# One decoder layer on one core: reordered ends of the sliding-window stage, block attention with one PSUM sum per tile, and a second place for one feed-forward factor

## The chip, the cores and the metric

The kernel is one program on one core of a Trainium2 chip. TensorE (PE) multiplies and transposes, VectorE (DVE), ScalarE (ACT) and GpSimd (POOL) work on tiles, SyncE (SP) and ACT issue the DMAs. The metric is the device time of one execution in microseconds (us). "Before" is the kernel without the change.

## The reference, cut to what matters

All data are float32, x is [1, 2048, 1024], one layer:

```
P = rms_norm(x) @ w_in                   # columns for the groups A (SWA), B (SSM), C (block attention)
A: 4 heads of 64, window 128, learned sinks, relative bias
B: S5 state-space model over 512 channels, then GELU and GLU
C: per query block of 128 (16 of them), 4 heads over one shared key/value head:
   o = g0 * softmax(q.k_cmp) v_cmp       # 127 compressed blocks; their probabilities pick the top 16 of 32 blocks
     + g1 * softmax(q.k_sel) v_sel       # keys of the selected blocks, others masked
     + g2 * softmax(q.k_win) v_win       # the last 512 keys
   k_cmp, v_cmp = gelu((blocks + pos) @ w1) @ w2
x = x + concat(rms_norm(o_A), rms_norm(o_B), rms_norm(o_C)) @ w_out
x = x + relu(rms_norm(x) @ w_up)^2 @ w_down      # w_up 1024 x 4096
```

## The kernel before, in words

A large product is made of three matmuls in fp32r (high x high, low x high, high x low; lines 76 to 78, and the same for the feed-forward at 1556 and 1738). Each operand is split in two: ACT writes the rounded high part, DVE the rest (`split`, lines 1414 and 1415).

*Front (0 to 418 us of the span).* x is normed and transposed, projected to the groups (`pm_a`, `pm_b`, `pm_c`, `pm_u`), and the state-space steps (`ssm_steps`) are merged between the last projection pieces; the last answer (`py`, lines 589 to 591) stands at the end.

*SWA, GLU, compress (418 to 611 us).* `merge` mixes three lists of steps in proportion: sliding-window attention, the GLU product of group B (`gpt` transposes, `gpm` products), and the preparation of group C with `compress_steps`. In the latter `cX` holds the tokens as two 512-column pieces, and `hidden` (line 765) reads it with a step of 8 elements: 16 fp32 matmuls `cph` of 129 columns per stream, two streams.

*Block attention and w_out (611 to 1304 us, `phase_mix`).* One tile is 128 queries. For each of three branches, `c` (compressed), `w` (window), `s` (selected): `logits` (line 875 on) makes q.k in PSUM (`pqc`, `pqw`, `pqs`; qA and qB are the two parts of the split query), DVE writes logits and their running maximum into a slab (`slc`, `slw`, `sls`, line 878; `nm..` is the last maximum), ACT takes the exponential of the whole slab and sums it (line 883, `den..`). `pv` transposes the slabs (`ppc`, `ppw`, `pps`, line 896), splits them (`th`, `tl`, lines 899 and 900), and multiplies by the values into a PSUM bank (`poc`, `pow`, `pos`, line 904). `combine` copies that bank to SBUF on ACT (`oT`, line 913), turns it back with four transposes (`pto.`, line 917), multiplies it by gate / denominator on DVE (`ot.`, line 919) and adds it to `oc` on POOL (lines 921 and 924). So each branch of each tile has its own bank, its own copy, four transposes, one DVE product and one to two POOL adds. A tile has four units: the heads 0 and 1, then 2 and 3, of `w`, then of `s`; the values of one unit are merged with the logits of the next unit. For tiles 8 to 15, `select` makes the mask of the top 16 blocks from the compressed probabilities; its transpose is `ptm` (line 1154), which goes into qB ahead of the selected logits. Between all this stand the products with w_out (`pw`, 48 matmuls per tile, placed with a priority offset), the norm of each finished tile (`xq`, `rr` on POOL), and the transposed rows for the feed-forward (`pth`).

*Feed-forward (1304 to 2572 us).* `phase_up` makes seven products per step in the manner of Strassen's method, in two halves of 16 steps f. The seven left factors ("1" to "7", order 1, 6, 7, 5, 2, 4, 3) are kept split in SBUF, one place for each. At the last step of half 0 each place is refilled for half 1 as soon as its product is done: "1" and "6" from fetched rows, the others landing by DMA in the place itself (`land`, then `split_landed`). `phase_down` follows.

The order on each engine comes from the order of these lists, from priority offsets (`late`), and from the pools, whose buffer counts decide what waits for a free place.

Of the kernel before, what the change touches and what calls it, by code (L numbers as in the profile page):

```python
# [80 lines left out]
def phase_front(tc, C, x, norm1_g, w_in, u_st, pd, rh_a, prm, dkp, dca, pre, extra, done):  # L81

    nc = tc.nc
    with ExitStack() as ctx:
# [165 lines left out]
        run(merge(rest, ssm_steps(tc, C, S, u_st, dkp, dca, tp, ps_g, ps_t)))  # L250
# [484 lines left out]
def compress_steps(tc, C, pool, tp, ps, pc, cmp_pos, cmp_w1, cmp_w2, gains):  # L735
# [7 lines left out]
    def start(st):  # L743
        X = box["X"] = tp.tile([P, 1040], F32, tag="X", name=f"cX{st}")
        nc.sync.dma_start(X[:, 1024:1040], cmp_pos[0, st].rearrange("(jj two) d -> (two d) jj", two=2))
        w1 = box["w1"] = tp.tile([P, 16, P], F32, tag="w1", name=f"cw1{st}")
        nc.sync.dma_start(w1, cmp_w1[0, st].rearrange("(jj p) f -> p jj f", p=P))
        w2 = box["w2"] = tp.tile([P, 64], F32, tag="w2", name=f"cw2{st}")
        nc.sync.dma_start(w2, cmp_w2[0, st])

    def turned(st, q):
# [6 lines left out]
        nc.scalar.copy(box["X"][:, 512 * q:512 * q + 512], pt.rearrange("p a b -> p (a b)"))  # L758

    def hidden(st):  # L760
# [3 lines left out]
        for jj in range(16):  # L764
            nc.tensor.matmul(ph, w1[:, jj], X[:, jj:jj + 8 * P + 1:8], start=jj == 0, stop=jj == 15)
# [80 lines left out]
class Attn:  # L846
# [12 lines left out]
    def logits(self, sl_of, h, qA, qB, chunks, m0, nm, den, name):  # L859
# [5 lines left out]
        def step(ci):  # L865
# [20 lines left out]
    def pv(self, po_of, sls_of, v_of, nblk, name):  # L886
# [3 lines left out]
        def step(b0):  # L890
            po, sls = po_of(), sls_of()
            nb = min(2, nblk - b0)
            pt = self.ps_p.tile([P, 2, 2, P], F32, tag="pp", name=f"pp{name}{b0}", bufs=2)
# [7 lines left out]
            for n, t in enumerate((th, tl)):  # L901
                with self.late(self.lag):
                    for j in range(nb):
                        nc.tensor.matmul(po, v_of(b0 + j), t[:, j].rearrange("p h q -> p (h q)"),  # L904
                                         start=b0 + j == 0 and n == 0, stop=b0 + j == nblk - 1 and n == 1)
        return [lambda b0=b0: step(b0) for b0 in range(0, nblk, 2)]

    def combine(self, po, w, acc, first, name, eng=None):
# [1033 lines left out]
```

## Time and profile before

| what | us |
|---|---|
| median of three runs | 2577.39 |
| lowest, highest run | 2571.80, 2578.93 |
| the profiled execution | 2574.28 |
| its span in the profile | 2572.5 |
| of which PE busy, DVE, ACT, POOL | 2475.1, 1769.6, 1324.9, 1119.3 |
| chain of waits: share spent on PE | 67% |

The profile is of one execution. Busy times of PE are sums over the stretches in which at least one matmul is in its pipeline, so short gaps between matmuls that depend on each other are partly counted as busy. A wait is put down to the semaphore that came last.

### The profile page before, as it was taken

What the parts mean: (1) busy time and instruction counts of PE and PEld (TensorE: products, weight loads), DVE (VectorE), ACT (ScalarE), POOL (GpSimd) and SP (SyncE); (2) the same over time, 40 slices, a digit from 0 to 9 for tenths busy, and PEclk for the clock granted to TensorE, in tenths of its full rate; (3) what the DMA queues carried; (4) which work ended last, traced back from release to release, by engine and by line L of the source; (5) the groups of instructions that cost most, each with busy time, mean ns of one, the idle gap of its engine ahead of it and who ended that gap; (6) DMA issues with size and microseconds to landing.
All of it is one profiled execution on the core that took longest, in us unless ns stands there. A gap on an engine that the chain in (4) does not pass through costs nothing.

```text
span 2572.5 us, 38493 instructions
## 1 busy us (share of the span) xinstructions
PE 2475.1 (96%) x12904; PEld 2080.1 (81%) x12904; DVE 1769.6 (69%) x3455; ACT 1324.9 (52%) x2767; POOL 1119.3 (44%) x1168
## 2 busy tenths in 40 slices
PE   8999998999999999999999999899999999999999
PEld 8989997777787777777777888688887888888887
DVE  4744876864787677777465565765557888888886
ACT  5334546765676565655465554544444444344442
POOL 3045222222223233332476767565545344454447
PEclk9999999999989999999999999999999999999999
DMA  6153426221212121221566667755547534444435
GB/s 199 61 126 102 116 89 172 86 60 50 65 64 71 36 67 48 87 66 56 177 204 187 187 185 207 233 163 144 153 130 251 167 93 136 132 132 130 123 98 197
DMA packets 397144, 324.66 MB, mean 126 GB/s; under 512 B 51943, under 2 KB 363885, under 8 KB 395121
## 3 DMA queue, kind: packets, MB, share of 16 engines
q1 hardware_dynamic: 360848, 297.03, 38.6%
q10 hardware_dynamic: 36096, 25.17, 3.1%
q8 instruction: 102, 1.67, 0.3%
q14 instruction: 98, 0.79, 0.1%
HBM read 209.66 MB, written 112.45 MB: 125 GB/s over the span
## 4 chain that ended last, share of the span: by engine, by line
PE 67%; DVE 5%; issue 2%; ACT 2%; DMA 2%; POOL 1%; SPq 0%; DVEq 0%; POOLq 0%; ACTq 0%
PE pdc L1738 7%; PE pdb L1738 7%; PE pda L1738 7%; PE pub L1556 6%; PE puc L1556 6%; PE pua L1556 6%; PE pdd L1738 3%; PE pud L1556 3%; PE pw L76 2%; PE pps L896 2%; PE pos L904 2%; PE pw L77 2%; PE pw L78 2%; DVE sls L878 1%; PE gpm L76 1%
## 5 line engine op out<-in xcount | busy, mean ns | idle before, releaser
L1414 ACT CAST v<-vr 128x512 fp32r<-128x512 f32 x224 | 139.4, 624 | 304.2 <-DMA vr<-vd 148.4
L1415 DVE TENSOR_TENSOR v<-vr,v 128x512 fp32r<-128x512 f32 x224 | 233.1, 1048 | 81.2 <-ACT v L1414 79.2
L1738 PE MATMUL pdc<-dw,v 128*128 128x512 f32 x768 | 187.0, 392 | 4.3 <-ACT dw L1414 3.2
L1738 PE MATMUL pdb<-dw,v 128*128 128x512 f32 x768 | 185.2, 390 | 0.0
L1738 PE MATMUL pda<-dw,v 128*128 128x512 f32 x768 | 184.5, 389 | 0.0
L1527 POOL TENSOR_TENSOR fs<-ur,ur 128x512 f32<-128x512 f32 x64 | 94.8, 1481 | 189.2 <-DMA ur<-in_w_up 152.0
L1738 PEld LDWEIGHTS pdc<-dw,v 128*128 128x128 f32 x768 | 145.3, 189 | 35.4 <-ACT dw L1414 3.7
L1738 PEld LDWEIGHTS pdb<-dw,v 128*128 128x128 f32 x768 | 144.8, 189 | 30.3
L1738 PEld LDWEIGHTS pda<-dw,v 128*128 128x128 f32 x768 | 144.1, 188 | 30.0
L1414 ACT CAST uh<-fs 128x512 fp32r<-128x512 f32 x128 | 78.5, 621 | 152.0 <-PE pub L1556 62.7
L1415 DVE TENSOR_TENSOR ul<-fs,uh 128x512 fp32r<-128x512 f32 x128 | 134.3, 1051 | 22.6 <-ACT uh L1414 22.3
L1415 DVE TENSOR_TENSOR ul<-ur,uh 128x512 fp32r<-128x512 f32 x96 | 101.0, 1053 | 52.3 <-ACT uh L1414 48.5
L900 DVE TENSOR_TENSOR tls<-pps,ths 128x512 fp32r<-128x512 f32 (+1 forms) x144 | 93.2, 658 | 46.0 <-ACT ths L899 37.7
L899 ACT CAST ths<-pps 128x512 fp32r<-128x512 f32 (+1 forms) x144 | 79.5, 565 | 83.4 <-PE pos L904 40.3
L76 PE MATMUL pw<-wo_h,mh 128*128 128x512 f32 x256 | 109.2, 427 | 6.2 <-ACT mh L1251 4.2
L1572 POOL TENSOR_TENSOR ev<-e,e 128x512 f32<-128x512 f32 x64 | 95.9, 1498 | 31.9 <-ACT e L1569 21.9
L1556 PE MATMUL pua<-fh,ul 128*128 128x512 f32 x256 | 100.9, 394 | 5.7 <-DVE ul L1415 5.7
L78 PE MATMUL pw<-wo_h,ml 128*128 128x512 f32 x256 | 105.4, 412 | 0.0
L77 PE MATMUL pw<-wo_l,mh 128*128 128x512 f32 x256 | 105.1, 410 | 0.0
L1556 PE MATMUL puc<-fh,uh 128*128 128x512 f32 x256 | 102.1, 399 | 1.9 <-DVE eu L1565 1.9
L1556 PE MATMUL pub<-fh,uh 128*128 128x512 f32 x256 | 102.1, 399 | 1.6 <-ACT fh L1414 1.6
L1556 PE MATMUL pua<-fh,uh 128*128 128x512 f32 x256 | 101.0, 395 | 2.5 <-ACT e L1576 2.5
(573 smaller groups left out, 7875.3 us busy)
## 6 DMA issues: line engine op xcount, KB each, us to landing
vr<-vd SPq DMA_DIRECT2D x224, 256.0 KB
ur<-in_w_up SPq DMA_DIRECT2D x128, 256.0 KB
vd<-ev SPq DMA_DIRECT2D x128, 256.0 KB
vd<-e ACTq DMA_DIRECT2D x64, 256.0 KB
dr<-in_w_down SPq DMA_DIRECT2D x32, 512.0 KB
x<-in_x SPq DMA_DIRECT2D x16, 512.0 KB
mx<-in_x SPq DMA_DIRECT2D x16, 512.0 KB
x<-mx ACTq DMA_DIRECT2D x16, 512.0 KB
```

Source lines behind the costliest of these rows:

```text
L76: nc.tensor.matmul(out, sh, mh, start=first, stop=False)
L77: nc.tensor.matmul(out, sh, ml, start=False, stop=False)
L78: nc.tensor.matmul(out, sl, mh, start=False, stop=last)
L896: nc.tensor.transpose(pt[:, j, hh], sls[hh][:, (b0 + j) * P:(b0 + j + 1) * P], C["ident"])
L899: nc.scalar.copy(th[:, 0:nb], pt[:, 0:nb])
L900: nc.vector.tensor_tensor(tl[:, 0:nb], pt[:, 0:nb], th[:, 0:nb], op=ALU.subtract)
L1414: nc.scalar.copy(dh, src)
L1415: nc.vector.tensor_tensor(dl, src, dh, op=ALU.subtract)
L1527: nc.gpsimd.tensor_tensor(t, x, y, op=op)
L1556: nc.tensor.matmul(bank[b], w[:, k], h[o][:, k], start=first and k == 0 and n == 0, stop=k == HALF - 1 and n == 2, skip_group_check=True)
L1572: nc.gpsimd.tensor_tensor(tile_("v" + o), x, y, op=op)
L1738: nc.tensor.matmul(bank[b, q], x[:, q, j], y[:, j], start=first and j == 0 and n == 0, stop=j == 1 and n == 2, skip_group_check=True)
```

## The change

1. Front: the last four projection pieces (48 matmuls `pm_c`) come after the last state-space step. The lists at the end of the SWA stage are merged in another proportion: six empty steps follow compress.
2. Compress: `cX` is laid out so that `cph` reads 129 neighbouring columns; ACT writes it in that layout, and the position row comes in two DMAs per stream.
3. Block attention: right after each exponential, DVE takes the reciprocal of that head's sum and POOL multiplies the whole slab by reciprocal x gate (line 887 of the changed kernel). All three branches then sum in one bank `poc` per tile, which a tile opens with its compressed values; one copy, four transposes and one DVE `tensor_reduce` give `oc`. The window slabs get a tag of their own. The values are merged with the logits of the unit after next. PSUM: three `pp` banks and one `po` bank instead of two and two.
4. Small edits in the same stage: two reciprocal square roots go from DVE to POOL, a square is written to SBUF instead of PSUM, `next_turned` stands later in the list of a tile.
5. Feed-forward: half 1's factor "1" has a place of its own (16 KB per partition), fetched and split at step 14; "6" and "7" are both refilled from fetched rows at step 15. One square per step goes from DVE to ACT.

```diff
-        run(merge(rest, ssm_steps(tc, C, S, u_st, dkp, dca, tp, ps_g, ps_t)))
+        run(merge(rest[:-4], ssm_steps(tc, C, S, u_st, dkp, dca, tp, ps_g, ps_t)) + rest[-4:])
...
-        nc.scalar.copy(box["X"][:, 512 * q:512 * q + 512], pt.rearrange("p a b -> p (a b)"))
+        nc.scalar.copy(box["X"][:, :, 64 * q:64 * q + 64], pt.rearrange("p a (m j) -> p j (a m)", j=8))
...
-            nc.tensor.matmul(ph, w1[:, jj], X[:, jj:jj + 8 * P + 1:8], start=jj == 0, stop=jj == 15)
+            nc.tensor.matmul(ph, w1[:, jj], X[:, jj % 8, jj // 8:jj // 8 + P + 1], start=jj == 0, stop=jj == 15)
...
                 nc.scalar.activation(x, x, AF.Exp, bias=nm[:, h:h + 1], scale=-1.0, accum_out=den[:, h:h + 1])
+                if gate is not None:
+                    nc.vector.reciprocal(den[:, h:h + 1], den[:, h:h + 1])
+                    nc.gpsimd.tensor_scalar(x, x, den[:, h:h + 1], gate, op0=ALU.mult, op1=ALU.mult)
...
+                        opening = b0 + j == 0 and n == 0 and first is not None
+                        begun = first.get("mm") if opening else None
+                        with self.tc.issue_after(begun) if begun is not None else nullcontext():
+                            mm = nc.tensor.matmul(po, v_of(b0 + j), t[:, j].rearrange("p h q -> p (h q)"), start=opening and begun is None,
+                                                  stop=last and b0 + j == nblk - 1 and n == 1, skip_group_check=True)
...
+        if w is None:
+            nc.vector.tensor_reduce(acc, pt.rearrange("p h a d -> p h d a"), axis=AX.X, op=ALU.add)
+            return
...
-        ps_p = pool("m_psp", 2, space=PSUM)
-        ps_o = pool("m_pso", 2, space=PSUM)
+        ps_p = pool("m_psp", 3, space=PSUM)
...
+        ps_o = pool("m_pso", 1, space=PSUM)
...
+                if i >= 8:
+                    pn = box["pn"] = lp.tile([P, 4, P], F32, tag="qd", name=f"pn{i}", bufs=1)
+                    nc.gpsimd.tensor_tensor(pn[:, :, 0:n], slc[:, :, 0:n], den.unsqueeze(2).broadcast_to([P, 4, n]), op=ALU.mult)
+                nc.gpsimd.tensor_tensor(slc[:, :, 0:n], slc[:, :, 0:n], w.unsqueeze(2).broadcast_to([P, 4, n]), op=ALU.mult)
...
-                def close(box=box, nm_=nm_, b=b, den=den, w=w):
-                    nc.vector.reciprocal(den, den)
-                    nc.vector.tensor_tensor(w, den, gt[:, :, b], op=ALU.mult)
-                    A.combine(box["po"], w, oc, False, f"{nm_}{i}", nc.vector if (nm_, i) == ("w", NT - 1) else None)
...
+                    if end and pair == 1:
+                        ps.append(lambda: A.combine(po(), None, oc, f"c{i}"))
...
+            for u in range(4):
+                if u == 2 and i + 1 < NT:
+                    ocs[i + 1] = box["oc"]
+                    nxt = units_of(i + 1, box)
...
+                new = cur[u + 2][0] if u < 2 else nxt[u - 2][0] if nxt else []
+                run(merge(cur[u][1], new, ahead[done_a:na], tail[done_t:nt]))
...
+        factors(ORDER[:1], "t")
+        second, hp["1"] = hp["1"], first
...
-                nc.vector.tensor_tensor(r, r, r, op=ALU.mult)
+                nc.scalar.activation(r, r, AF.Square)
...
+            if (p, f) == (0, NF - 2):
+                hp["1"] = second
+                fetch_factor(1, "1")
             if last:
-                for o in ORDER[:2]:
+                for o in ORDER[1:3]:
                     fetch_factor(1, o)
...
+                if (p, f) == (0, NF - 2) and k == 4:
+                    again = refill(1, "1")
```

What stands on PE between the front and the SWA stage, in the kernel before (`py15` is the last answer of the state-space steps, `pm15_c` the last projection piece, `ptqa` a transpose of SWA queries that POOL makes as `qda`, `bpfs` the bias of SWA, `gpt` transposes for the GLU; the last digits are running numbers of the program):

```order
L78 MATMUL pm15_c0_4856<-wh_c0_7_4323,hl15_2484 128x396
L589 MATMUL py15_4895<-Wc15_4787,U15_4802 128x256
L590 MATMUL py15_4895<-Wc15_4787,U15_4802 128x128
L591 MATMUL py15_4895<-CA15_4786,St1_3076 128x256
L589 MATMUL py15_4895<-Wc15_4787,U15_4802 128x256
L590 MATMUL py15_4895<-Wc15_4787,U15_4802 128x128
L591 MATMUL py15_4895<-CA15_4786,St1_3076 128x256
L712 MATMUL bpfs0_4983<-Ts_4981,c_anti_4936 128x512
L647 MATMUL gpt0_5084<-c_ident_60,z0_5082 128x128 x3
L825 MATMUL ptqa0_4994<-c_ident_60,qda0_4992 128x128 x3
```

And in the changed kernel, from the last projection piece on:

```order
L78 MATMUL pm15_c0_4872<-wh_c0_7_4383,hl15_2484 128x396
L647 MATMUL gpt0_5084<-c_ident_60,z0_5082 128x128 x4
L712 MATMUL bpfs0_4983<-Ts_4981,c_anti_4936 128x512
L647 MATMUL gpt1_5472<-c_ident_60,z1_5470 128x128 x2
L712 MATMUL bpfs2_4986<-Ts_4981,c_anti_4936 128x512
L647 MATMUL gpt1_5472<-c_ident_60,z1_5470 128x128 x2
L712 MATMUL bpf00_5058<-T0_5056,c_anti_4936 128x512
L76 MATMUL gpm01_5509<-glu_h_4974,zh0_5089 128x512
L77 MATMUL gpm01_5509<-glu_l_4975,zh0_5089 128x512
L78 MATMUL gpm01_5509<-glu_h_4974,zl0_5090 128x512
L76 MATMUL gpm01_5509<-glu_h_4974,zh0_5089 128x512
L826 MATMUL ptqa0_4994<-c_ident_60,qda0_4992 128x128 x4
```

The answer has moved ahead of the last projection pieces, and products of the GLU stand between them and the first SWA transpose.

On DVE, in block attention at tile 12 of the changed kernel, after the logits of head 0 of the selected branch (`nms12` its maximum, written by the rows of line 879; `qB1` is the low part of tile 13's query, `kAs` the keys):

```order
L879 ISA sls120_13200,nms_12852<-pqs1203_13269,b_sel_4941,mx_13199 128x512
L879 ISA nms_12852 128x1
L904 TENSOR_TENSOR tlw1200_13286<-ppw1200_13280,thw1200_13285 128x512
L833 SCALAR_TENSOR_TENSOR qB1_7405<-ptqc13_13299,gains_62,qA13_13304 64x512
L879 ISA sls121_13329,mx_13328<-pqs1210_13330,b_far_4945 128x512
L879 ISA mx_13328 128x1
L886 RECIPROCAL dens_12853<-dens_12853 128x1
L839 SCALAR_TENSOR_TENSOR kAs_7400<-ptkc13_13307,gains_62,kAs_7400 64x128
```

In the kernel before one reciprocal of all four heads stood at the end of the branch; here each head has its own, three operations behind its maximum.

On DVE at the change of halves in the feed-forward (`fl16` is the low part of factor "6" of half 1, `ul105` the low part of weights of half 1 for product "5", `e` and `eu` results of products), in the kernel before:

```order
L1415 TENSOR_TENSOR fl11_19047<-fx11_19027,fh11_19046 128x2048
L1565 TENSOR_TENSOR eu2015_19063<-pud015_19050,e1015_19031 128x512
L1415 TENSOR_TENSOR fl16_19066<-fx16_19029,fh16_19065 128x2048
L1565 TENSOR_TENSOR eu3015_19082<-puc015_19069,eu2015_19063 128x512
L1415 TENSOR_TENSOR ul106_19203<-fs102_19200,uh106_19202 128x512
L1565 TENSOR_TENSOR e22015_19100<-pub015_19087,eu3015_19082 128x512
L1415 TENSOR_TENSOR ul107_19209<-fs103_19206,uh107_19208 128x512
L1415 TENSOR_TENSOR ul105_19213<-fs101_19198,uh105_19212 128x512
L1415 TENSOR_TENSOR fl17_19085<-fl17_19085,fh17_19084 128x2048
L1592 TENSOR_TENSOR e11015_19110<-e11015_19110 128x512
L1565 TENSOR_TENSOR e21015_19143<-puc015_19069,eu2015_19063 128x512
L1415 TENSOR_TENSOR fl15_19106<-fl15_19106,fh15_19105 128x2048
```

And in the changed kernel:

```order
L1575 TENSOR_TENSOR eu2015_18864<-pud015_18851,e1015_18836 128x512
L1421 TENSOR_TENSOR ul106_19003<-fs102_19000,uh106_19002 128x512
L1421 TENSOR_TENSOR fl16_18867<-fx16_18832,fh16_18866 128x2048
L1575 TENSOR_TENSOR eu3015_18883<-puc015_18870,eu2015_18864 128x512
L1421 TENSOR_TENSOR fl17_18886<-fx17_18834,fh17_18885 128x2048
L1575 TENSOR_TENSOR e22015_18902<-pub015_18889,eu3015_18883 128x512
L1421 TENSOR_TENSOR ul107_19009<-fs103_19006,uh107_19008 128x512
L1421 TENSOR_TENSOR ul105_19013<-fs101_18998,uh105_19012 128x512
L1421 TENSOR_TENSOR ul102_19017<-ur1012_18992,uh102_19016 128x512
L1575 TENSOR_TENSOR e21015_18943<-puc015_18870,eu2015_18864 128x512
L1421 TENSOR_TENSOR fl15_18908<-fl15_18908,fh15_18907 128x2048
```

The split of "1" is gone from here (it stands some thirty rows earlier), that of "7" reads fetched rows (`fx17`) and stands ahead of the weight splits, and the square of line 1592 is on ACT.

## Rows read from the trace of the kernel before

**Rows 1.** The page: span, and (columns: engine, busy us, share, instructions) the busy line.

```profile
span 2572.5 us, 38493 instructions
...
PE 2475.1 (96%) x12904; PEld 2080.1 (81%) x12904; DVE 1769.6 (69%) x3455; ACT 1324.9 (52%) x2767; POOL 1119.3 (44%) x1168
```

**Rows 2.** Stages of the program as windows (columns: window, its length, then busy us of PE, PEld, DVE, ACT, POOL with the count of instructions, granted clock of PE as a share of full speed, DMA share, GB/s). In order: front; SWA, GLU and compress; block attention and w_out; up; down.

```profile
0.00:418.00 418.00, 402.37 (x2584) 385.14 (x2584) 247.12 (x608) 194.90 (x403) 120.07 (x200) 1.00 0.40 116
418.00:611.00 193.00, 175.88 (x985) 140.35 (x985) 125.88 (x377) 123.36 (x376) 49.42 (x54) 0.98 0.32 93
611.00:1304.00 693.00, 651.51 (x3898) 536.26 (x3899) 497.77 (x1449) 420.90 (x1023) 235.31 (x467) 0.97 0.24 75
1304.00:1951.00 647.00, 632.90 (x2753) 512.42 (x2752) 387.42 (x425) 330.54 (x560) 403.42 (x274) 0.99 0.61 178
1951.00:2572.50 621.50, 612.47 (x2688) 505.87 (x2686) 511.37 (x600) 255.24 (x407) 311.07 (x175) 0.99 0.47 146
```

**Rows 3.** PE in block attention, 611 to 1304 us, by groups (columns: line, engine, operation, out<-in, shapes, count; busy us and mean ns of one; idle us just before them and what ended it).

```profile
L76 PE MATMUL pw<-wo_h,mh 128*128 128x512 f32 x256 | 109.2, 427 | 6.2 <-ACT mh L1251 4.2 <-DVE ml L1252 1.4 <-ACT pw L1267 0.3
...
L896 PE MATMUL pps<-c_ident,sls 128*128 128x128 f32 x544 | 93.1, 278 | 4.5 <-DVE tls L900 2.0 <-ACT sls L883 1.4 <-DVE rat L52 0.3
...
L875 PE MATMUL pqs<-kAs,qA 128*128 128x512 f32 (+3 forms) x160 | 66.1, 413 | 7.2 <-DVE mx L878 5.6 <-DVE nms L878 1.0 <-DVE nmc L878 0.3
...
L896 PE MATMUL ppw<-c_ident,slw 128*128 128x128 f32 x280 | 57.0, 292 | 1.7 <-DVE nmc L878 0.7 <-ACT slw L883 0.5 <-DVE tls L900 0.2
...
L1249 PE MATMUL ptx<-c_ident,mix 128*128 128x128 f32 x128 | 20.8, 286 | 3.3 <-ACT pw L1267 1.7 <-DVE ml L1252 1.3 <-ACT mx L1287 0.2
...
L1284 PE MATMUL pth<-c_ident,mx 128*128 128x128 f32 x64 | 12.4, 287 | 2.9 <-POOL mx L1276 2.9
L917 PE MATMUL ptos<-c_ident,oTs 128*128 128x128 f32 x64 | 11.2, 291 | 2.0 <-ACT oTs L913 1.9
L917 PE MATMUL ptow<-c_ident,oTw 128*128 128x128 f32 x64 | 10.8, 279 | 0.2
```

**Rows 4.** The chain of waits, 505 to 625 us (columns: start us, us, engine, tile, line, count).

```profile
507.77 0.44 PE ptoa L917 x4
...
521.35 7.64 PE cph L765 x32
...
584.01 3.37 issue
...
588.12 7.74 PE cph L765 x32
```

**Rows 5.** Two fp32 products, all their matmuls (columns: line, engine, operation, out<-in, count; shortest/median/longest ns; first and last start; form). The first has neighbouring columns, the second a step of 8.

```profile
L590 PE MATMUL py<-Wc,U x64: 272/274/275, 266.9 to 416.3; 128*128 128x128 f32 x64
...
L765 PE MATMUL cph<-cX,cw x64: 412/413/478, 521.3 to 595.4; 128*128 128x129 f32 x64
```

**Rows 6.** ACT, then DVE in block attention, by groups (columns as in Rows 3).

```profile
L883 ACT ACTIVATE sls<-sls,nms 128x128 f32<-128x128 f32 (+15 forms) x64 | 77.5, 1211 | 23.6 <-DVE nms L878 21.9 <-DVE im L1146 1.6
L883 ACT ACTIVATE slw<-slw,nmw 128x640 f32<-128x640 f32 (+4 forms) x64 | 49.0, 766 | 19.5 <-DVE nmw L878 19.3
...
L883 ACT ACTIVATION_READ_ACCUMULATOR sls<-sls,nms 128x1 f32 x64 | 12.5, 195 | 0.0
...
L913 ACT COPY oTs<-pos 128x512 f32<-128x512 f32 x16 | 9.4, 585 | 3.7 <-PE pos L904 3.6
...
L919 DVE TENSOR_TENSOR ots<-ptos,ws 128x512 f32<-128x512 f32 x16 | 11.0, 687 | 6.1 <-PE ptos L917 6.1
...
L1141 DVE TENSOR_REDUCE pm<-pn 128x72 f32<-128x288 f32 (+7 forms) x8 | 7.0, 871 | 1.5 <-POOL pn L1140 1.3
...
L1129 DVE RECIPROCAL denc<-denc 128x4 f32<-128x4 f32 x16 | 2.8, 173 | 1.3 <-ACT slc L883 1.1
```

**Rows 7.** POOL in block attention, by groups (columns as in Rows 3).

```profile
L924 POOL TENSOR_TENSOR oc<-oc,ots 128x256 f32<-128x256 f32 x32 | 23.5, 735 | 79.9 <-DVE ots L919 77.0 <-DVE denw L1182 1.7
L924 POOL TENSOR_TENSOR oc<-oc,otw 128x256 f32<-128x256 f32 x30 | 22.6, 754 | 41.9 <-DVE otw L919 25.7 <-DVE wc L1132 9.3 <-DVE im L1145 3.8
...
L921 POOL TENSOR_TENSOR oc<-otc 128x256 f32<-128x256 f32 x16 | 11.8, 735 | 82.2 <-DVE otc L919 82.2
...
L1276 POOL TENSOR_SCALAR mx<-mx,rr 128x1024 f32<-128x1024 f32 x8 | 8.9, 1118 | 0.8
...
L1239 POOL TENSOR_SCALAR mix<-mix,r_a 128x256 f32<-128x256 f32 x16 | 7.6, 477 | 2.6 <-DVE r_c L54 2.6
```

**Rows 8.** Four windows of 20 us: the start of the SWA stage, and the change of halves (columns as in Rows 2).

```profile
420.00:440.00 20.00, 14.49 (x72) 10.17 (x73) 15.33 (x45) 16.40 (x45) 6.21 (x5) 0.91 0.80 214
1600.00:1620.00 20.00, 20.00 (x89) 16.25 (x88) 12.91 (x12) 12.93 (x18) 15.02 (x10) 1.00 0.55 152
1620.00:1640.00 20.00, 18.51 (x79) 14.47 (x78) 13.22 (x12) 9.94 (x12) 8.43 (x5) 1.00 0.85 311
1640.00:1660.00 20.00, 11.81 (x43) 8.86 (x42) 20.00 (x17) 10.62 (x15) 12.83 (x7) 0.83 0.73 225
```

**Rows 9.** The change of halves: a row of the chain of waits, then rows of the order of events on DVE (columns: start us, us, engine, line, operation, out<-in, count, and in brackets the idle time before it).

```profile
1624.77 6.03 DMA fl<-sums
...
1632.77 2.29 DVE L1415 TENSOR_TENSOR fl<-fl,fh 128x2048 fp32r<-128x2048 f32 x1 [6.78 <-ACT fh L1414]
...
1642.86 3.35 DVE L1415 TENSOR_TENSOR fl<-fl,fh 128x2048 fp32r<-128x2048 f32 x1
```

More of the change, by code (lines that the diff above doesn't have):

```diff
@@ L743, in start @@
     def start(st):
-        X = box["X"] = tp.tile([P, 1040], F32, tag="X", name=f"cX{st}")
-        nc.sync.dma_start(X[:, 1024:1040], cmp_pos[0, st].rearrange("(jj two) d -> (two d) jj", two=2))
+        X = box["X"] = tp.tile([P, 8, 130], F32, tag="X", name=f"cX{st}")
+        for b in range(2):
+            nc.sync.dma_start(X[:, :, 128 + b], cmp_pos[0, st, 16 * b:16 * b + 16].rearrange("(jj two) d -> (two d) jj", two=2))
         w1 = box["w1"] = tp.tile([P, 16, P], F32, tag="w1", name=f"cw1{st}")
@@ L857, in late, with logits @@
         return self.tc.high_priority(offset=-n) if n else nullcontext()
-    def logits(self, sl_of, h, qA, qB, chunks, m0, nm, den, name):
+    def logits(self, sl_of, h, qA, qB, chunks, m0, nm, den, name, gate=None):
         nc = self.nc
@@ L1118, in slab @@
                 return slc
-            def po():
-                if "po" not in box:
-                    box["po"] = ps_o.tile([P, 512], F32, tag="po", name=f"poc{i}")
-                return box["po"]
             res = []
@@ L1266, in out @@
                     box["ss"] = small(2, "xs")
-                nc.scalar.activation(pw, xt, AF.Square, accum_out=box["ss"][:, n:n + 1])
+                nc.scalar.activation(late["fp"].tile([P, 512], F32, tag="sq", name=f"xsq{i}{n}"), xt, AF.Square, accum_out=box["ss"][:, n:n + 1])
                 if n == 1:
@@ L1315, in finish_steps @@
             res = [load, lambda: turned(0, 4), lambda: turned(4, 8)] + [lambda n=n, k=k: filler(n, k) for n, k in order]
+            before = late.pop("turn", [])
+            res[8:8] = before
             if i >= NT // 2:
-                res.insert(8, blocks)
-                res.insert(13, block_sums)
-            res[1:1] = late.pop("turn", [])
+                res.insert(8 + len(before) * 3, blocks)
+                res.insert(13 + len(before) * 3, block_sums)
             if i < NT // 2:
@@ L1329, in front, with po @@
             box = {}
+            def po():
+                if "po" not in box:
+                    box["po"] = ps_o.tile([P, 512], F32, tag="po", name=f"poc{i}")
+                return box["po"]
+            box["po_of"] = po
             def start():
@@ L1446, in phase_up @@
         factors(ORDER[3:])
+        first = hp["1"]
+        factors(ORDER[:1], "t")
+        second, hp["1"] = hp["1"], first
         ps_u = pool("f_psu", 2, space=PSUM)
@@ L1504, in refill @@
         def refill(p, o):
-            hh[o], hl[o] = (hp[o].tile([P, HALF, 4, P], F32R, tag=n + o, name=f"f{n}{p}{o}") for n in "hl")
-            split(nc, hh[o], hl[o], rows.pop(o))
+            t = [hp[o].tile([P, HALF, 4, P], F32R, tag=n + o, name=f"f{n}{p}{o}") for n in "hl"]
+            split(nc, *t, rows.pop(o))
+            return t
         def weights(p, f):
@@ L1616, in phase_up @@
             if k < 2:
-                refill(0, o)
+                hh[o], hl[o] = refill(0, o)
             else:
```

108 lines of the change are left out of this document (47 added, 61 removed).

## The prediction

> **What bounds the kernel.** I read the stages first [rows 2]. PE is busy in 402 of 418 us, 176 of 193, 652 of 693, 633 of 647 and 612 of 622; no other engine comes near, the closest being DVE in block attention with 498 of 693. PE's order is the bound everywhere, and a change pays in two ways: work that PE no longer does, and gaps on PE that close. The visible gaps are 16, 17, 41, 14 and 9 us. Two stages have most of them, so I looked at those two group by group [rows 3] and at the chain through the stage before them [rows 4]. In the feed-forward one place stands out: of the windows of 20 us [rows 8] a full one holds 89 matmuls, and the two at the change of halves hold 79 and 43. That is 56 missing, and at 20/89 = 0.225 us each 12.6 us, nearly the whole gap of that stage.
>
> The sum is made against the profiled execution, 2574.28 us, of which the span is 2572.5 [rows 1]; the median of the three runs is 3 us higher, their lowest 2.5 us lower.
>
> **Block attention, removed work on PE.** Two of three turns per tile go: 2 x 16 x 4 = 128 transposes (`ptos`, `ptow`, 64 each [rows 3]). Four of them in a row take 0.44 us when nothing holds them, the first of [rows 4], so 32 x 0.44 = 14.1 us of PE's order. They also waited 2.0 and 0.2 us for the copies. This is -16 and nearly sure, because it stands on the engine that bounds.
>
> **Block attention, waits that may close.** The values now come two units behind the logits. Waiting for the slab or its split parts cost the transposes `pps` 4.5 and `ppw` 1.7 us [rows 3]; the part of these that hangs on the exponential should go, the part that hangs on `tls` (2.0) not. PE's wait of 7.2 us before `pqs` is for DVE to free the logits' bank, and DVE is hardly lighter: it loses 48 products of 0.687 us (33 us) and small products and reciprocals of 14 us at most (64 at about 0.2), and gains 128 reciprocals of at most 0.173 (22 us) and 16 reduces of about 0.87 (14 us) [rows 6]. That is 498 - 33 - 14 + 22 + 14 = 487 us. ACT loses 32 copies of 0.585, 19 of 421 us [rows 2, 6], which frees the casts a little. For these waits I take -4, with bounds of -25 (all of the 41 us of gaps but the 16 that I ascribe to other causes, the logits and w_out) and +20 (below).
>
> **Block attention, the new work on POOL.** The gates multiply all slabs. Window slabs have min(i+1, 5) blocks of 128, selected ones i+1, times four heads: 35,840 and 69,632 elements per partition over 16 tiles. POOL's products with a scalar took 477 ns at 256 elements and 1118 at 1024 [rows 7]: 0.835 ns per element over about 0.263 us fixed. So 128 x 0.263 + 105,472 x 0.000835 = 34 + 88 = 122 us. The 16 products of the compressed slabs add about 10 (from the adds of 0.735 for 256 elements). Gone are 11.8 + 23.5 + 22.6 = 58 us of adds. POOL goes from 235 to about 309 of 693 us, 45%. It is hidden by the distance of two units, except where a gate queues behind POOL's chain for a finished tile (eight small operations and a product of 1.118) or where three gates of late tiles of 1.5 to 2 us follow one another. A missed one costs PE one or two us unless w_out products fill in. I take +2, bounds 0 and +15.
>
> **Block attention, single bank and selection.** With one `po` bank, the first compressed value of a tile must wait for the copy of the tile before (0.585 us [rows 6] plus the drain of the last product). That happens 15 times, with w_out products to fill: +3, bounds 0 and +12. In the order of the changed kernel the mask of tiles 8 to 15 stands close in front of its logits; eight times a part of a chain of small DVE operations: +2, bounds 0 and +8. The edits of group 4 take the square away from the bank that w_out waits for (`ptx` 1.7 us, `pw` 0.3, both on ACT `pw`) and let `mx` be ready before `pth` (2.9) [rows 3]: -3 of 4.9, bounds -5 and +2. The moved square roots are small and early; POOL's queue hides them, and uncovered they would cost a few us once.
>
> Block attention sums to -16 - 4 + 2 + 3 + 2 - 3 = -16. Since the waits that the profile names hide drains which it counts as busy (four transposes that wait for a copy take the bank, the copy and the turn in sequence), I put it at -22, with -50 and +8 as ends. The addition of 6 is judgement: every dependent step that is taken off PE's order lets its neighbours pipeline.
>
> **Compress.** The 64 `cph` take 413 ns, a contiguous fp32 product of nearly the same size 274 [rows 5]; their two runs on the chain took 7.64 + 7.74 = 15.4 us [rows 4]. If the step of 8 elements is what makes the difference, 64 x 0.139 = 8.9 us go; the odd 129th column keeps a little, so -8. If it is the odd column itself, nothing goes: bounds -9 and 0. The writes of ACT now scatter, eight of them, off the chain.
>
> What decides between the two is a rule: the Trainium skill, "SBUF — State Buffer", section "Door 1: The DMA port swizzle", states that SBUF is read in lines of 16 bytes and that each access to a new line pays. The step of 8 fp32 values is 32 bytes, a new line each time. By that rule the sum has -8, without it 0. The longer `cph` rows agree with it but don't exclude the odd column.
>
> **Front and SWA.** PE is busy for 14.49 of the first 20 us at a granted clock of 0.91 [rows 8], waiting for queries that POOL and DVE prepare. In the new order GLU products stand there, work that came later anyway; the last answer is made earlier, so its `z` is there. I take -3 of the 5.5 us. The 3.37 us of issue ahead of the second `cph` [rows 4] is a wait for loads that the earlier placing may hide: -2. Bounds for both together -9 and +3 (the projection pieces now end later, and the stores and loads of SWA's tiles stand behind them on SP's queue).
>
> **Change of halves.** PE waits there for DVE, which is busy for all 20 us from 1640 [rows 8]. It stood idle for 6.78 us before 1632.77, because the split of "7" waited for a DMA of 6.03 us [rows 9], and then did splits of 2.28 to 3.35 us. Now "1" is split thirty rows earlier, and "7" from rows fetched early, ahead of the DMA wait. One split (2.3 to 3.4) leaves the crowded stretch, the idle 6.8 us are used by the split of "7" and the weights behind it, and one square goes to ACT. What is late next is "5", which lands by a DMA of the same length after its own product, one product of 12 x 0.225 = 2.7 us later; but half 1 asks for it only after the products of "1", "6" and "7", 8 us into the half. I take -8 of 12.6, bounds -12 and +1. The 32 squares on ACT cost 0.6 us each beside 331 of 647 us of ACT's work: nothing, unless a wait is behind them. The fetch of "1" lies two steps before its use.
>
> The border between block attention and the feed-forward changes its order on ACT: 0, bounds -4 and +4.
>
> **Sum.** -22 - 8 - 5 - 8 = -43, so 2574.3 - 43 = 2531; the medians lie 3 us above the profiled execution, and I say 2532.
>
> **Rivals.**
> *Only the sure terms.* The transposes with their waits (-16), half of the compress term (-4) and of the change of halves (-4), the rest cancelled by POOL's and DVE's new waits: 2574 - 24 = 2550. For it speaks that DVE stays at 70% in block attention, and PE's longest named wait (`pqs`) is for DVE. Chance 0.18.
>
> *The gaps close.* With two units between logits and values PE runs nearly without gaps: block attention -50, the other terms at their good ends (-9, -9, -12) give 2574 - 80 = 2494. For it speaks that 41 us of gaps stand in rows 2; against it that one third of them belong to DVE's freeing of banks. Chance 0.15.
>
> *The reciprocals park DVE.* Each stands three operations behind its head's maximum, some 2 us of DVE, while the exponential takes 1.211 + 0.195 or 0.766 us [rows 6] once ACT is free. If ACT is behind by as much, DVE waits in order: at worst 64 x 1.4 + 64 x 0.96 = 151 us, and with the logits' sums and the splits `tls` queued behind it, PE waits. DVE at 487 + 151 = 638 of 693 would be a second bound. It is slower than before if PE pays over half of the 151: +75 instead of -4 - 6, so -43 + 85 = +42, 2616. It decides from about 50 us of PE waits. Against it: ACT is at 61% in that stage, and waited 22 and 20 us in total for these maxima, that is, it usually stands ready. Chance 0.06.
>
> *DVE slows the gates.* If DVE's instructions held POOL up and the gates took twice as long, POOL would stand at 309 + 122 = 431 of 693 us and the last three gates of a late tile at 3 to 4 us each; with 2 us of PE's time lost per tile the forecast becomes 2532 + 32 = 2564. Against it: the three groups of adds that POOL has now in this stage, beside a DVE that is 72% busy, take 735, 735 and 754 ns [rows 7], even to 3%. Chance 0.04. Beside it stands a rule that speaks against this change: the Trainium skill, "SBUF — State Buffer", section "Who interferes with whom", says that a DVE instruction with two SBUF inputs contends with a GpSimd instruction that reads SBUF; it gives the condition, and the DVE groups here mostly read PSUM with one operand (`tls<-pps,ths`).
>
> *The change does not do what it says at the change of halves:* "5" takes the place of "7" as what DVE and PE wait for, and the stall stays. 2532 + 8 = 2540; inside the range. Chance 0.1.
>
> **How the numbers follow.** My forecast has 0.47. A measurement of this kernel can tell about 0.3%, 7.7 us. Faster by more: the forecast, the sure terms, closed gaps and the stalled halves (0.90) and part of the slowed gates, 0.89 after tails. Same: the rest of the slowed gates and the tail of the sure terms, 0.05. Slower: parked DVE, 0.06. Range: from closed gaps at 2494 down to 2488, and above the sure terms to 2566. The forecast's own range is 2510 to 2550.
>
> **What would show it.** In block attention the stage lasts about 671 instead of 693 us, `ptos` and `ptow` are gone, POOL's busy time is near 309 and the gates' mean near 0.95 us. `cph` has a mean near 274 ns. The windows at the change of halves hold over 75 matmuls each. Wrong it is if DVE shows long waits on ACT at line 886, if PE waits for POOL's line 887 for more than 10 us, or if `poc` waits for the copy of line 913's successor.

## The result and the profile after

The changed kernel takes 2548.57 us (median of four, 2545.77 to 2552.13), the kernel before 2576.38 in the same runs: ratio 0.9896, 95% interval 0.9883 to 0.9908, that is 27 us faster. The forecast was 2532 in a range of 2488 to 2566: the sign and the range held, the gain is about 60% of what was forecast.

The profiled execution took 2552.13 us, the longest of the four. The page's span of the changed kernel, and its stages as windows (columns as in [rows 2], which they answer to; the borders are where the last projection, the first product of `phase_up` and the first of `phase_down` lie):

```profile
span 2550.2 us, 38303 instructions
...
0.00:417.00 417.00, 400.90 (x2586) 384.05 (x2586) 254.19 (x612) 196.67 (x407) 122.56 (x200) 1.00 0.40 114
417.00:611.00 194.00, 175.75 (x996) 137.00 (x996) 132.56 (x425) 128.69 (x410) 53.56 (x64) 0.94 0.36 99
611.00:1291.00 680.00, 625.30 (x3757) 528.34 (x3756) 475.48 (x1396) 398.59 (x954) 320.47 (x554) 0.96 0.25 77
1291.00:1929.00 638.00, 629.88 (x2754) 510.54 (x2753) 347.24 (x391) 345.74 (x592) 395.62 (x271) 1.00 0.62 179
1929.00:2550.20 621.20, 612.49 (x2688) 505.46 (x2686) 512.37 (x600) 254.95 (x407) 310.98 (x175) 0.99 0.47 146
```

Block attention is 13 us shorter and `phase_up` 9; front, SWA and `phase_down` are as before (one execution against one; the last section shows how far two of them can differ). But PE sits idle in block attention for 680 - 625 = 55 us, where it was 41 [rows 2]: less work and more gaps. Which gaps, the groups of PE there show (columns as in [rows 3]):

```profile
L76 PE MATMUL pw<-wo_h,mh 128*128 128x512 f32 x256 | 109.7, 428 | 7.6 <-ACT mh L1250 5.8 <-ACT mx L1286 0.6 <-DVE mx L1263 0.5
...
L900 PE MATMUL pps<-c_ident,sls 128*128 128x128 f32 x542 | 102.1, 281 | 9.1 <-POOL sls L887 5.4 <-DVE tls L904 3.5
...
L911 PE MATMUL poc<-tls,Vs 128*128 128x256 f32 x272 | 64.8, 302 | 5.4 <-DVE tls L904 5.4
L876 PE MATMUL pqs<-kAs,qA 128*128 128x512 f32 (+3 forms) x156 | 64.1, 411 | 1.6 <-DVE mx L879 0.7 <-DVE nms L879 0.4
...
L1248 PE MATMUL ptx<-c_ident,mix 128*128 128x128 f32 x128 | 21.1, 285 | 4.2 <-DVE mx L1263 3.1 <-POOL mix L1238 0.7 <-DVE ml L1251 0.4
...
L900 PE MATMUL ppc<-c_ident,slc 128*128 128x128 f32 x60 | 13.8, 285 | 4.4 <-POOL slc L1140 4.4
...
L1283 PE MATMUL pth<-c_ident,mx 128*128 128x128 f32 x64 | 10.8, 293 | 7.3 <-DVE mx L1263 6.8 <-ACT mx L1286 0.2
```

`ptos` and `ptow` are gone. The wait of `pqs` for DVE fell from 7.2 to 1.6 us. In their place stand waits that were not there: 5.4 for a gate on POOL, 4.4 for the compressed slab on POOL, 5.4 for `tls`, and 6.8 of `pth` for DVE's add. The first is one single wait. POOL and, in the middle, DVE in the order of events ahead of it (columns as in [rows 9]):

```profile
692.48 0.16 DVE L886 RECIPROCAL dens<-dens 128x1 f32<-128x1 f32 x1
```

```profile
696.80 0.39 POOL L52 TENSOR_TENSOR rat<-rat,rah 128x16 f32<-128x16 f32 x2
697.18 0.47 POOL L941 TENSOR_SCALAR mix<-oc,nr 128x256 f32<-128x256 f32 x1
697.62 0.36 POOL L53 TENSOR_SCALAR rat<-rat 128x16 f32<-128x16 f32 x2
697.95 0.22 POOL L54 TENSOR_TENSOR r_a<-r_a,rat 128x16 f32<-128x16 f32 x1
698.13 0.22 POOL L54 TENSOR_TENSOR r_c<-r_c,rat 128x16 f32<-128x16 f32 x1
698.43 0.20 POOL L1072 TENSOR_SCALAR r_c<-r_c 128x16 f32<-128x16 f32 x1
698.62 0.77 POOL L887 TENSOR_SCALAR sls<-sls,dens,gt 128x512 f32<-128x512 f32 x1
```

The gate at 698.62 had its reciprocal at 692.64. For 6 us it stood behind 27 small steps: the moved square roots (`rat`, `r_a`, `r_c`) and a tile's norm. The wait for `tls` at 1065 us is of the same kind, one step removed. DVE, then POOL:

```profile
1058.03 0.69 DVE L904 TENSOR_TENSOR tls<-pps,ths 128x512 fp32r<-128x512 f32 x1 [0.30 <-ACT ths L903]
1063.79 0.93 DVE L1147 TENSOR_REDUCE pm<-pn 128x112 f32<-128x448 f32 x1 [5.07 <-POOL pn L1139]
1064.63 1.28 DVE L904 TENSOR_TENSOR tls<-pps,ths 128x512 fp32r<-128x512 f32 x2
```

```profile
1058.57 0.34 POOL L48 TENSOR_SCALAR nqt<-nr,nqh 128x1 f32<-128x1 f32 x1
...
1061.99 0.87 POOL L887 TENSOR_SCALAR slw<-slw,denw,gt 128x640 f32<-128x640 f32 x1
1062.82 0.93 POOL L1139 TENSOR_TENSOR pn<-slc,denc 128x448 f32<-128x448 f32 x1
```

DVE stands 5.07 us in front of the selection's reduce, which waits for `pn`; `pn` stands on POOL behind one column-sized step after another (some 0.4 us from start to start) and a gate; and `tls`, which waits for nothing on POOL, stands behind the reduce on DVE. PE waits for `tls`.

### The profile page after: what moved, and what is told of

Its sections match the earlier page's. It is cut to its first block, busy times and chain, and to the rows that moved or that the text cites. A ratio compares the mean times of both kernels' runs of the same rounds, so it can differ in the third digit from the quotient of the medians.

```text
span 2550.2 us, 38303 instructions
## 1 busy us (share of the span) xinstructions
PE 2444.3 (96%) x12776; PEld 2065.4 (81%) x12776; DVE 1721.8 (68%) x3424; ACT 1324.6 (52%) x2767; POOL 1203.2 (47%) x1263
## 4 chain that ended last, share of the span: by engine, by line
PE 63%; DVE 5%; DMA 3%; POOL 3%; issue 3%; ACT 2%; SPq 0%; ACTq 0%; DVEq 0%; POOLq 0%
PE pdc L1755 7%; PE pdb L1755 7%; PE pda L1755 7%; PE pub L1566 6%; PE puc L1566 6%; PE pua L1566 6%; PE pdd L1755 3%; PE pud L1566 3%; PE poc L911 3%; PE pps L900 2%; PE pw L76 2%; PE pw L77 2%; PE pw L78 2%; PE pqs L876 1%; PE pqs L877 1%
## 5 line engine op out<-in xcount | busy, mean ns | idle before, releaser
L1421 DVE TENSOR_TENSOR ul<-ur,uh 128x512 fp32r<-128x512 f32 x96 | 93.3, 972 | 109.8 <-ACT uh L1420 109.7
L887 POOL TENSOR_SCALAR sls<-sls,dens,gt 128x128 f32<-128x128 f32 (+15 forms) x64 | 81.7, 1277 | 105.8 <-DVE dens L886 85.7
L900 PE MATMUL pps<-c_ident,sls 128*128 128x128 f32 x544 | 103.0, 281 | 9.1 <-POOL sls L887 5.4
L887 POOL TENSOR_SCALAR slw<-slw,denw,gt 128x640 f32<-128x640 f32 (+4 forms) x64 | 52.9, 827 | 122.1 <-DVE denw L886 98.5
```

What stands on the lines that cost most here:

```text
L887: nc.gpsimd.tensor_scalar(x, x, den[:, h:h + 1], gate, op0=ALU.mult, op1=ALU.mult)
L900: nc.tensor.transpose(pt[:, j, hh], sls[hh][:, (b0 + j) * P:(b0 + j + 1) * P], C["ident"])
L1421: nc.vector.tensor_tensor(dl, src, dh, op=ALU.subtract)
```

## The experiments

First each part of the change alone on the kernel before. The diffs are the parts of the change itself. *The feed-forward alone:*

> The kernel before with the feed-forward part of the change alone. Theory: the change of halves is a local stall, so it gives its -9 us (the up stage got 9.2 us shorter in the changed kernel) whatever stands ahead of it: ratio 0.9965, up stage 638 us. Rival: part of the 9.2 us is the border to block attention, which has moved too: then under 6 us here.

2569.04 against 2573.85, ratio 0.9992 (0.9980 to 1.0005; these ratios are nearer to those of the means than of the medians): between nothing and 5 us, not the theory's 9 and within the rival's "under 6". Seven of the ten runs lie between 2566.51 and 2570.20 us and three above 2576.8; the profiled execution, 2577.20, is one of the three, so what it shows need not hold for the seven. In it the stall at the change of halves still stands. PE in 20 us there, then ACT at the split of "5":

```profile
1635.00:1655.00 20.00, 14.50 (x54) 10.69 (x54) 14.76 (x11) 13.89 (x16) 8.32 (x4) 0.91 0.71 244
```

```profile
1636.74 1.92 ACT L1414 CAST fh<-fl 128x2048 fp32r<-128x2048 f32 x1 [6.84 <-DMA fl<-sums]
```

54 matmuls of 89 are 35 missing, 7.9 us, where [rows 8] had 12.6 in two windows. ACT waits 6.84 us for "5" to land; in the changed kernel the same cast waits 2.38 us, and there the load is issued 4.2 us after the split of "7" (1607.37 against 1603.13), here 7.5 us after it (1629.30 against 1621.84). So the rival forecast as "5 takes the place of 7" is what happened in this execution, and mostly not in that of the changed kernel. The rest of the change does not by itself keep it away, for it stands again in the profile of the changed kernel with three chains moved (below), which has the same feed-forward code:

```profile
1600.00:1620.00 20.00, 15.78 (x54) 11.82 (x53) 18.08 (x16) 12.15 (x18) 14.70 (x8) 0.83 0.69 207
```

```profile
1592.65 1.91 ACT L1420 CAST fh<-fl 128x2048 fp32r<-128x2048 f32 x1 [6.21 <-DMA fl<-sums]
```

Why the load is issued later there was not settled. The split of "1", which comes ahead of its rows, costs something here too: ACT waits 7.55 us for them, and the window of 20 us from 1555 holds 74 matmuls.

The rival of this run, the border, has a number in the run of block attention below, which has no edit of the feed-forward: from the first `pua` to the first `pda` its up stage takes 643.1 us (1290.0 to 1933.1), against 647.2 before, 638.0 in the changed kernel and 646.5 here. So about 4 of the 9 us may come with the border; these are single profiles.

*Compress alone:*

> The kernel before with the new layout of the compress tokens alone. Theory: the 64 matmuls drop from 413 to 275 ns and stand on the chain, so the program is 7 to 9 us shorter: ratio 0.997. Rival: the SWA stage waits for other engines, and what PE gains there it waits later: under 3 us.

2567.49, ratio 0.9978 (0.9968 to 0.9988), 5.7 us (3.1 to 8.2): the rival's "under 3 us" is out, the theory's 7 to 9 just reached by the interval. The product before and in the changed kernel among the groups of PE (columns as in [rows 3]), then its durations in the changed kernel (as in [rows 5]):

```profile
L765 PE MATMUL cph<-cX,cw 128*128 128x129 f32 x64 | 15.5, 416 | 0.8 <-DVE ga L670 0.8
```

```profile
L766 PE MATMUL cph<-cX,cw 128*128 128x129 f32 x64 | 7.7, 278 | 0.0
...
L766 PE MATMUL cph<-cX,cw x64: 272/275/377, 500.1 to 562.0; 128*128 128x129 f32 x64
```

413 became 275 ns with the same 129 columns: the step was the cost, not the odd column. This agrees with the rule of the Trainium skill ("SBUF — State Buffer", "Door 1: The DMA port swizzle") that each access to a new line of 16 bytes pays. PE's order got 15.5 - 7.7 = 7.8 us back, not 64 x 0.138 = 8.8, because these matmuls overlap; by the ratio about three quarters of it reach the end.

*Block attention alone:*

> The kernel before with the block-attention part alone (gates, one bank, two units, small edits). Theory of the queue: POOL's queue in order gives back about 15 us, so this part is worth only 8 to 14 us: ratio 0.995 to 0.997, with waits of PE for POOL's gate and slab products of 10 to 15 us. Rival: this part is worth 20 us or more (ratio under 0.992), and the reordered ends of the SWA stage gave some of it back.

2559.64, ratio 0.9949 (0.9934 to 0.9964), 13 us: the theory of the queue, and the three waits of PE are there again (the lines lie one ahead of those of the changed kernel):

```profile
700.06 0.47 PE L899 MATMUL pps<-c_ident,sls 128*128 128x128 f32 x1 [5.40 <-POOL sls L886]
719.31 1.11 PE L899 MATMUL ppc<-c_ident,slc 128*128 128x128 f32 x4 [4.58 <-POOL slc L1139]
1065.21 0.79 PE L910 MATMUL poc<-tls,Vs 128*128 128x256 f32 x2 [4.56 <-DVE tls L903]
```

*The ends alone:*

> The kernel before with the reordered ends of the front and of SWA alone. Theory of the queue: about nothing, within 4 us either way. Rival: slower by 6 us or more, since the last SWA product came 6.6 us later in the changed kernel and the granted clock of that stage fell from 0.98 to 0.94.

2578.82, ratio 1.0026 (1.0010 to 1.0042): 6.7 us slower (2.6 to 10.8), nearer to the rival's 6 than to nothing. The four ratios multiply to 0.9945 (0.9918 to 0.9972 by their intervals together) or -14 us, the whole change has -27: the parts do not add. So the next runs undo or mend one thing in the changed kernel.

*The front's end undone in the changed kernel:*

```diff
-        run(merge(rest[:-4], ssm_steps(tc, C, S, u_st, dkp, dca, tp, ps_g, ps_t)) + rest[-4:])
+        run(merge(rest, ssm_steps(tc, C, S, u_st, dkp, dca, tp, ps_g, ps_t)))
```

> The changed kernel with the front's last four projection pieces merged back among the state-space steps. Theory of SP's queue: in the changed kernel the first loads of SWA's rows are issued at 419.5 us, behind the last store of the projection, 4.4 us later than before, and POOL makes the first queries 6.5 us later; with the order back the first SWA transpose comes at about 420 us and the program is 4 to 7 us faster than the changed kernel: 2541 to 2545 us. Rival: PE only swaps waits there, GLU products fill either way: within 2 us.

2549.27, ratio 0.9907 (0.9891 to 0.9923): the same as the changed kernel. The mechanism is in the trace, the loss is not. In the changed kernel SP issues the first load of SWA's rows at 419.52 and POOL makes the queries at 424.90; before, at 415.13 and 418.42:

```profile
419.52 0.75 SPq L961 DMA_DIRECT2D ta<-pa  x1
```

```profile
424.90 1.47 POOL L819 TENSOR_TENSOR qda<-ta,rh_a 128x768 f32<-128x768 f32 x1 [0.67 <-DMA ta<-pa]
```

*The six empty steps taken out of the changed kernel* (`b_nsa + c_steps` without the `[lambda: None] * 6`):

> The changed kernel without the six empty steps behind compress. Theory of SP's queue: these only shift compress against SWA, within 3 us of the changed kernel. Rival: they take steps of SWA's end away from its cover, and their removal is worth what the ends cost, 5 us or more.

2551.26, ratio 0.9919 (0.9905 to 0.9934): the same or a little slower. So neither half of the ends, undone by itself, gives anything back in the whole change, though both together cost 6.7 us on the kernel before; both at once were not undone in the changed kernel. The theory of SP's queue falls as an account of the time.

*Three chains from POOL to DVE in the changed kernel:*

```diff
-            rsqrt_into(nc, sm, ra, ss_a, 1.0 / 256, NT, "ra", nc.gpsimd)
+            rsqrt_into(nc, sm, ra, ss_a, 1.0 / 256, NT, "ra")
...
-        rsqrt_into(nc, self.sm, r, ss, 1.0 / 256, 1, "nq", eng)
+        rsqrt_into(nc, self.sm, r, ss, 1.0 / 256, 1, "nq", nc.vector)
...
-                    nc.gpsimd.tensor_tensor(pn[:, :, 0:n], slc[:, :, 0:n], den.unsqueeze(2).broadcast_to([P, 4, n]), op=ALU.mult)
+                    nc.vector.tensor_tensor(pn[:, :, 0:n], slc[:, :, 0:n], den.unsqueeze(2).broadcast_to([P, 4, n]), op=ALU.mult)
```

> The changed kernel with three things taken off POOL and given to DVE: the two reciprocal square roots of 16 columns, the small operations of each tile's norm (the scale stays on POOL), and the product for the selection (pn). Theory of POOL's queue: the three long waits of PE (5.4 for a gate, 4.4 for the compressed slab, 5.2 for a split held up by pn) go, about 15 us in the profile, and the program is 8 to 14 us faster than the changed kernel: 2535 to 2541 us. Rival: DVE, which gets about 30 us more, then holds the logits and PE waits for it instead: within 4 us.

2531.59, ratio 0.9830 (0.9812 to 0.9849) against 0.9896 (0.9883 to 0.9908) of the changed kernel: 17 us faster (by the two intervals 11 to 23), more than expected. Block attention as one window, then the longest waits of PE in it (columns: what waited, for what, us in total, times, longest):

```profile
611.00:1268.00 657.00, 619.41 (x3745) 520.62 (x3744) 495.09 (x1546) 396.31 (x951) 275.49 (x395) 0.98 0.25 80
```

```profile
PE pth L1283 <- DVE mx L1263: 5.3, 4, 1.9
PE pqw L876 <- DVE nmc L879: 3.2, 2, 1.6
PE poc L911 <- DVE tlw L904: 3.2, 5, 1.2
...
PE ppc L900 <- POOL slc L1140: 1.0, 2, 0.6
```

The waits for the gate, for `slc` (4.4 to 1.0) and for `tls` behind `pn` are gone. DVE is at 495 of 657 us, 75%, and PE waits for it hardly more: DVE had room, POOL's order had not. The gates themselves stayed on POOL. The clock does not make the difference: its mean over the four runs is 0.988 against 0.987, by estimate 3 us at most (0.001 of 2550 us). Two of the three chains, each tile's norm and `pn`, stood on POOL before the change too; PE waited for POOL for 3.2 us in all in block attention then, against 10.5 in the changed kernel. Moving them in the kernel before was not tried, so what part of the 17 us is a price of the change, and what part would have been there without it, is not shown.

*Of these, the square roots alone back on DVE* (the first line of that diff and its twin for `rc`):

> The changed kernel with only the two reciprocal square roots of 16 columns back on DVE. Theory of POOL's queue: the 5.4 us wait of PE for a gate at 694 to 699 us goes and nothing else does: 4 to 6 us faster than the changed kernel, 2543 to 2545 us. Rival: the wait is one of several at that place (loads of w_out, the clock) and only moves: within 2 us.

2544.46, ratio 0.9882 (0.9861 to 0.9902): 3.6 us by the ratios, its interval overlaps the changed kernel's, so the size is not sure. In the profile the 5.4 us wait and the 4.4 for `slc` are gone; one of 2.9 for a gate and one of 3.2 for a maximum on DVE (`nmw`) have come.

*The feed-forward's transposes back at the start of a tile's list* (`res[1:1] = late.pop("turn", [])`):

> The changed kernel with the transposes for the feed-forward back at the start of a tile's list. Theory of the one bank: they wait there for the DVE add that empties the bank of the w_out product (6.8 us, and 3.1 for the transposes behind it), and these waits fall to about the 3 us that POOL's scale cost before: 3 to 6 us faster. Rival: the place was no cost, the wait moves: within 2 us.

2547.06, ratio 0.9904 (0.9889 to 0.9918): the same. The waits move, as the rival said:

```profile
PE pw L76 <- DVE mx L1263: 5.3, 5, 2.3
...
PE pth L1283 <- POOL mx L1275: 4.1, 6, 1.7
```

One PSUM bank serves `ptx`, `pw` and `pth`; whichever comes after the add waits for it.

*The split of "1" held back.* In the changed kernel's up stage two windows of 20 us fall short, one of them at a place that was full before, and ACT parks there:

```profile
1544.00:1564.00 20.00, 17.17 (x75) 13.72 (x74) 10.32 (x12) 11.29 (x18) 5.32 (x4) 1.00 0.82 256
1624.00:1644.00 20.00, 16.70 (x73) 13.24 (x72) 18.21 (x14) 10.45 (x17) 15.52 (x8) 1.00 0.69 208
```

```profile
1546.72 1.91 ACT L1420 CAST fh<-fx 128x2048 fp32r<-128x2048 f32 x1 [7.46 <-DMA fx<-hT]
```

14 and 16 of 89 matmuls are missing, 3.1 and 3.6 us. The edit ties the split to an instruction of step 13:

```diff
-                    again = refill(1, "1")
+                    with tc.issue_after(done[NF - 3]):
+                        again = refill(1, "1")
```

(`done` holds the squares of product "2", one per step.)

> The changed kernel with the split of half 1's factor "1" held back until the last product of step 13 has been squared (it had been placed about 1.3 steps earlier, right behind the load of its rows). Theory of the parked split: in the changed kernel ACT stands 7.5 us for these rows with the weight splits queued behind it, and PE loses 3.1 us there; this goes, the change of halves stays as it is, and the program is 2 to 4 us faster than the changed kernel: 2544 to 2547 us. Rival: the two later fetches now start later, and the change of halves loses the same again: no change.

2543.61, ratio 0.9872 (0.9852 to 0.9892). The place is full again, the change of halves pays a part back:

```profile
1536.00:1556.00 20.00, 20.00 (x88) 16.25 (x88) 10.91 (x13) 10.06 (x17) 9.60 (x8) 1.00 0.71 223
1616.00:1636.00 20.00, 16.65 (x66) 13.10 (x65) 17.52 (x17) 10.91 (x20) 14.09 (x8) 0.91 0.79 237
```

At the halves 7 more matmuls are missing in this window than before the edit (66 against 73), and 4 more in the one ahead of it (84 against 88): 2.5 of the 3.1 us. From the first `pua` to the first `pda` the stage takes 636.9 us against 638.0. The ratio says 6 us, with an interval that overlaps the changed kernel's; in the two profiles the difference stands ahead of this stage (last section). So the theory holds for the place, and the time that it promised is not shown.

*The same with the front's end undone:*

> The kernel without the last four pieces at the front's end, and with the late split of "1". Theory of SP's queue with the parked split: undoing the front's end gave 5.8 us up to the first feed-forward product, which the parked split (8.4 us of loss in that run, 3.1 in the changed kernel) took back; with the late split both are kept and the time is 2538 to 2543 us. Rival: the front's order is worth nothing, as its timed runs say, and this equals the late split alone.

2547.52, ratio 0.9890 (0.9872 to 0.9907): not faster than the late split alone. The rival holds: the front's order is worth nothing here. The 5.8 us of the theory were the first product of `phase_up`, at 1285.0 us in the profile with the front undone and 1290.8 in that of the changed kernel; the late split alone, with the changed front, has it at 1283.0. So the 5.8 us lie within what one program shows from execution to execution.

*All together:*

> The changed kernel with the three chains on DVE, the front's end and the place of the feed-forward transposes as before the change, and the late split of "1". Theory: the parts lie in different stages and add up: 17 (chains, measured) + 6 (front) + 2 (transposes) + 3 (split) = 28 us below the changed kernel, 2518 to 2526 us. Rival: the gains overlap, since the chains' part has taken the waits of the same stretch: 2526 to 2532 us, no better than the chains alone.

2527.99, ratio 0.9814 (0.9796 to 0.9832), the fastest kernel of the study: 47 us under the kernel before and about 21 under the changed one. It lies at the rival's end: beyond the chains (0.9830) nothing is certain to have been added.

## Why the prediction was right, and where it was wrong

**Right: what bounds, and the removed work.** PE is the bound. 128 transposes and both sets of waits for the copies went, and PE's wait of 7.2 for the logits' bank fell to 1.6. I had left that last one at nothing, saying DVE was hardly lighter; DVE went to 475 of 680 us, and what did the rest (the larger distance between logits and values would be one reason) no run took apart.

**Wrong: "It is hidden by the distance of two units ... I take +2, bounds 0 and +15" (the new work on POOL), and "POOL's queue hides them" (the square roots).** This is the step that failed. The size of the work was near: 122 us forecast, and on the page after the two groups of gates have

```profile
L887 POOL TENSOR_SCALAR sls<-sls,dens,gt 128x128 f32<-128x128 f32 (+15 forms) x64 | 81.7, 1277 | 105.8 <-DVE dens L886 85.7
...
L887 POOL TENSOR_SCALAR slw<-slw,denw,gt 128x640 f32<-128x640 f32 (+4 forms) x64 | 52.9, 827 | 122.1 <-DVE denw L886 98.5
```

that is 135 us, and POOL is busy for 320 of 680 us (47%), 309 of 693 forecast. I had named the case, a gate behind the chain of a finished tile, and put it at one or two us a time and +2 in all. A busy share of 47% says nothing of how long due work stands in an order: a gate stood behind 27 steps, `pn` behind some ten, of 0.2 to 0.5 us each, and the three waits are 15 us. Taking three such chains away was worth 17 us; that the forecast was off by nearly as much (16.6) is partly chance, since the ends, the halves and compress fell short as well. My sign of being wrong, over 10 us of PE's waits for line 887, did not show (5.4), because the rest stands under `slc` and `tls`.

**Wrong: selection, +2.** I looked for the cost in the mask's distance to its logits. It was one stage earlier, on DVE's order behind `pn`: 5.2 us at one tile.

**Right in size, not by its working: compress.** The forecast took 64 durations of 139 ns off, but these matmuls overlap: 64 x 413 ns are 26 us, and the chain had 15.4. The order of PE got 7.8 us back, near the -8; the time moved by 5.7 (3.1 to 8.2).

**Wrong in sign or unproven: the ends, -5.** Alone they cost 6.7 us; in the whole they cost or give nothing that the runs can tell. The prediction named the delay (stores ahead of SWA's loads) and put it at +3 at most.

**Half right: the halves, -8.** In the changed kernel's profile 12.6 us became 3.6, but the hoisted split of "1" parked ACT and cost 3.1 that I had not seen: "The fetch of "1" lies two steps before its use" is true of the use, not of the split. With the same feed-forward code in the kernel with three chains moved, the stall at the halves is back. Alone on the kernel before, the part gave between nothing and 5 us.

**The small edits, -3 of 4.9.** `pth` and `ptx` waited 2.9 and 3.3 before and wait 7.3 and 4.2 after: +5.3 in the waits, and moving them back gains nothing. At the border `pw` waits 5.8 for `mh` where it was 4.2.

**The rivals.** The time lies at the upper end of the forecast's own 2510 to 2550 and on "only the sure terms" (2550), to which I gave 0.18, and for its reason, new waits for POOL and DVE. "The reciprocals park DVE": DVE stood 14.5 + 11.3 us behind the exponentials at line 886, not 151, and PE's waits for DVE's logits fell. "DVE slows the gates": they are 10% over the estimate (135 for 122), far from double.

Why the parts alone make 14 us and the whole 27 is not settled. The ends cost 6.7 us alone and nothing in the whole that undoing one half would show. For the feed-forward the profiles differ by the later load of "5", which comes and goes between executions; no run took that part out of the changed kernel.

## What to carry to other kernels

Before work is moved to an engine with a low share, list what stands ahead of it in that engine's order at the moment it is due: a chain of small dependent steps holds up everything due behind it, and one wait in the middle does the same, also for what needs nothing from there. When a gain falls short, look for new waits of the bound engine and follow each back to the first engine that was late; then move the short chain, not the long work. A split or a load that a scheduler hoists parks its engine until the data lands, so check where it ends up, not where it was written.

## What the hardware showed unexpectedly

The granted clock differs between executions of the same code. The changed kernel and the one with the late split have the same program, in the same order on every engine, up to the middle of `phase_up`. The same 40 us in each, the changed kernel first:

```profile
597.00:617.00 20.00, 18.84 (x77) 15.34 (x77) 13.20 (x68) 11.85 (x52) 8.77 (x16) 0.66 0.15 41
577.00:597.00 20.00, 18.47 (x92) 13.58 (x91) 8.36 (x19) 8.24 (x25) 6.68 (x11) 1.00 0.26 80
```

```profile
597.00:617.00 20.00, 18.03 (x98) 13.85 (x97) 14.30 (x74) 13.40 (x57) 11.18 (x22) 1.00 0.14 41
577.00:597.00 20.00, 18.46 (x95) 13.89 (x94) 8.21 (x25) 9.02 (x31) 6.19 (x11) 1.00 0.25 80
```

PE was equally busy ahead of it (18.47 and 18.46 of 20 us, at a granted clock of 1.00, which is 2.4 GHz), and then the one execution spent much of 20 us at 1.2 GHz and did 77 matmuls, the other none of it and did 98. The first `pqs` of line 876 lies at 601.78 us in the one and 599.96 in the other, the fifth at 617.91 and 611.63: 4.5 us more in that stretch. By the first product of `phase_up` the two are 7.8 us apart (1290.8 and 1283.0). So a difference of a few us between two profiles is no proof of an edit, and the parts of that size are judged by the timed runs.
